# Window outputs of a hybrid encoder layer kept on chip, their norm and output projection begun in the last window units

## The chip, the core and the metric

The kernel runs on one core of one Trainium2 chip. TensorE (PE) does the matmuls, VectorE (DVE), ScalarE (ACT) and GpSimd (POOL) the elementwise work, SyncE (SP) issues most of the DMAs between HBM and the on-chip memories (SBUF, and PSUM where matmuls accumulate). The metric is device time in microseconds (us) of one execution, as a median of several runs.

## What is computed

One layer on 1024 tokens with 16 meta tokens ahead (L = 1040), width 1024, fp32. Two SwiGLU blocks stand around a mixer with two kinds of heads:

```
h += 0.5 * SwiGLU_1(RMSNorm(h))
z  = RMSNorm(h) @ W_in
     group A: 4 differential heads  a = softmax(q0 k0) - lam * softmax(q1 k1);  a @ v;  RMSNorm per head
     group B: sliding window (+-128 tokens, 16 meta keys), 8 query heads, 2 kv heads, a sink logit per head
h += concat(A, RMSNorm(B)) @ W_out
h += 0.5 * SwiGLU_2(RMSNorm(h));  out = RMSNorm(h)[16:]
```

The change lies in group B: its output (512 channels x 1024 tokens) has to be normed over its 512 channels, multiplied with the second half of W_out, and added to the residual h.

## The kernel before, in words

Each fp32 operand is cut into a rounded high part (a cast on ACT, L117) and a low part (a subtraction on DVE or POOL, L114), and a product is three matmuls, high by high, low by high and high by low (`mm3`, L163 to L169). Activations lie with channels on the 128 partitions and tokens along the free axis. A weight tile is loaded, cast and subtracted by `load_w` (L171). The order of instructions on each engine is not written out: when the program is built, a scheduler that plays a model timeline orders the engines' queues, within what pools and their buffers allow. So the text of the program and the order in a queue differ, and a pool with fewer buffers can hold work back.

The stages around the change, in time order:

- **Units** (L1019). 16 window units (2 kv heads x 8 token blocks of 128) are run with the projections that are still missing: `fillers` (L913) hands out projection matmuls (`pj`) between the unit's own. A unit is `win_scores` (L936: matmuls to `ws`, masked row maximum on DVE, exp on ACT to the tile `p4`, division on POOL) and, one unit later, `win_values` (L978: transposes to `wt`, cut into thi and tlo, matmuls with the values to `wo`, at L1007 and L1008 a copy and an addition to the output tile `ow`). L1009 writes `ow` to HBM, to the tensor `ow_d`. At i == 13 the projections are drained, the pools of differential heads opened, and `load_head(0)` (L728) loads head 0: keys and queries come from HBM (`kraw`, `qraw`), are cast on ACT and cut on POOL (`kl` L114, `qst` L743).
- **Head loop** (L1181). 4 differential heads x 8 query blocks are 32 steps, and 4 steps to drain. The first three score steps are drawn into units 14 and 15 (`EARLY`). A step is `scores` (L756: 12 matmuls `ds` for each of the two softmaxes, a row maximum on DVE L767, exp on ACT L769), `combine` one step later (POOL L776, DVE L777), `transposes` two steps later (`dt`, copied out on DVE and ACT), and on even steps from 4 on `values` (L1161). The odd steps from 9 on take one **tile** of `out_win` (L1128): 12 matmuls of 512 columns for one 128-row block m of the output and one half c of the tokens, of the window part of W_out, with the addition to h (`hrm`) and a write to `h2_d`. There are 16 such tiles, in the order m, then c; a weight block is loaded once for two tiles. 14 fit into the odd steps, two stand behind the loop.
- **Window norm** (`win_norm`, L1089), at step 4 for the first token half and at step 8 for the second: 1 MB is read back from `ow_d` into `own`, squared on ACT, summed over the four tiles by three additions on POOL (L1073), summed over partitions by one ones-matmul (L1075), then `rsqrt` (L1078; the activation function's table is exchanged for it and back), and four times a multiplication on POOL (L1095), a scaling on ACT (L1097) and a low part on DVE (L1098) give `ow_hi` and `ow_lo`.
- **Head norm** (`head_norm`, L1114) at steps 7, 11, 15, ... for half a head each.
- **Output projection** of the differential heads (`prepare2`, L1238): 16 tiles `po` of 12 matmuls, whose weight blocks 0 and 1 have buffers of the pool `owp`, open since before the loop; then the norm of the second FFN (`first_half`, `combine2`), beside which the first products of that FFN run (`lead`, L254, whose weights come by `rg<-wg`, L257).

Of the kernel before, what the change touches and what calls it, by code (L numbers as in the profile page):

```python
# [10 lines left out]
F32 = mybir.dt.float32  # L11
# [30 lines left out]
N_EARLY = sum(len(v) for v in EARLY.values())  # L42
DNG = 3
# [8 lines left out]
def layer(  # L52
# [10 lines left out]
    class Rings:  # L63
# [5 lines left out]
        def reserve(self, tag, bufs=1):  # L69
            pools = [self.stack.enter_context(mk_pool(f"{self.name}_{tag}{i}", side=self.side, space=self.space)) for i in range(bufs)]  # L70
            self.tags[tag] = [pools, 0]
            return self
# [650 lines left out]
    ow_d = dpool.tile([P, 4, SEQ], F32, name="ow_d")  # L723
# [4 lines left out]
    def load_head(hd):  # L728
        khs, kls, qs = [], [], []
        for c in range(2):  # L730
# [16 lines left out]
        v = kp.tile([P, NB + 1, P], F32, tag="v", name="v", bufs=2)  # L747
# [8 lines left out]
    def scores(head, qt, c, tiles, ds):  # L756
# [11 lines left out]
        p = dp.tile([P, L], F32, tag=f"dp{c}", name=f"dp{c}", bufs=3)  # L768
# [11 lines left out]
    pend, sc = {}, {}  # L780

    with ExitStack() as st:
# [63 lines left out]
        st_h.close()  # L846
        vpool2 = st.enter_context(mk_pool("vbp"))
# [130 lines left out]
        def win_values(kv, n, p4):  # L978
# [4 lines left out]
            for j in range(nk + 2):  # L983
# [22 lines left out]
            ow = wp.tile([P, 512], F32, tag="ow", name="ow")  # L1006
            nc.scalar.copy(tmp[mine, :], po[other, :])  # L1007
            nc.vector.tensor_tensor(ow[mine, :], po[mine, :], tmp[mine, :], op=ALU.add)  # L1008
            nc.sync.dma_start(  # L1009
                ow_d[mine, :, n * P : (n + 1) * P], ow[mine, :].rearrange("p (g q) -> p g q", g=4)  # L1010
# [8 lines left out]
        for i, (kv, n) in enumerate(units):  # L1019
# [5 lines left out]
            if i == 13:  # L1025
# [4 lines left out]
                for tag, bufs in (("v", 2), ("qst", 3), ("kh", 3), ("kl", 3), ("kraw", 1), ("qraw", 1)):  # L1030
                    kp.reserve(tag, bufs)
                dp = Rings(st_k, "dp", "right", bufs=2)
                for tag, bufs in (("dp0", 3), ("dp1", 3), ("at", 2), ("oh", 2)):
                    dp.reserve(tag, bufs)
# [15 lines left out]
    h2_d = [[dpool.tile([P, 512], F32, name=f"h2_{m}_{c}") for c in range(2)] for m in range(KT)]  # L1050
    st_o = ExitStack()
# [3 lines left out]
    owp = Rings(st_o, "ow").reserve("owraw").reserve("owhi", 2).reserve("owlo", 2)  # L1055
    with ExitStack() as st:
        op = Rings(st, "op").reserve("ow_hi").reserve("ow_lo")
        npool = Rings(st, "dn")
# [3 lines left out]
        ow_hi = op.tile([P, 4, SEQ], F32R, name="ow_hi")  # L1062
        ow_lo = op.tile([P, 4, SEQ], F32R, name="ow_lo")

        def sums(srcs, n):
            acc = npool.tile([P, 512], F32, tag="nacc", name="nacc")[:, :n]
            for i, s in enumerate(srcs):
                if i == 0:
                    nc.scalar.activation(acc, s, AF.Square)
                else:  # L1070
                    sq = npool.tile([P, 512], F32, tag="nsq", name="nsq")[:, :n]
                    nc.scalar.activation(sq, s, AF.Square)
                    nc.gpsimd.tensor_tensor(acc, acc, sq, op=ALU.add)  # L1073
            ps = psum.tile([P, 512], F32, tag="do", name="do")[:, :n]
            nc.tensor.matmul(ps, ones, acc, start=True, stop=True)  # L1075
            return ps

        def rsqrt(v, n, width):  # L1078
            r = npool.tile([P, SEQ], F32, tag="nr", name="nr")[:, :n]
# [318 lines left out]
```

## Time and profile before

| | us |
|---|---|
| median of 3 runs | 2109.07 |
| lowest, highest | 2106.53, 2112.87 |
| the profiled execution, its own time | 2112.15 |
| its span | 2110.4 |
| PE busy in the span | 1947.8 (92%) |
| DVE, POOL, ACT busy | 1304.6 (62%), 1042.0 (49%), 877.2 (42%) |
| mean granted TensorE clock | 0.974 of 2.4 GHz |

The page lists busy time for each engine over the whole span. It is an average over stages: the two FFNs take most of the span with PE near its limit, and PE's row of 40 slices shows its lowest full slices, 7 tenths, at slices 21 and 22 (1055 to 1161 us) and 27 and 28 (1372 to 1477 us), ahead of and behind the head loop. A stage is therefore read by itself: what each engine was busy in it, what the chain of waits names in it, and what single instructions wait for. The stages are the units (870 to 1043 us), a hand-over from the last units to step 9 of the head loop (1043 to 1151), the rest of that loop (to 1337), the output projection (to 1399) and the norm of the second FFN (to 1453). In a row of a timeline the first number is the start, the second the duration in us, and square brackets hold the idle time of the engine just before it and what ended it; 128x512 and the like are partitions x elements.

### The profile page before, as it was taken

The numbers are of one execution on the slowest core, as the hardware profiler recorded it, in microseconds if no ns is written. First come the engines' busy times: TensorE is split into PE (matmuls) and PEld (weight loads), VectorE is DVE, ScalarE is ACT, GpSimd is POOL, SyncE is SP. The second block draws the span as 40 slices with busy tenths as digits, with TensorE's granted clock in tenths as the row PEclk, the third lists the DMA queues.
The fourth block names the chain that finished last, engine by engine and source line by source line (L and its number), as shares of the span: only waits on it lengthen the run. The fifth ranks groups of instructions, "written<-read, shape, count | busy, mean of one in ns | idle before, by whom it ended". The sixth has DMA issues, their size and how long they took to land.

```text
span 2110.4 us, 30362 instructions
## 1 busy us (share of the span) xinstructions
PE 1947.8 (92%) x11484; PEld 1695.8 (80%) x11484; DVE 1304.6 (62%) x1804; ACT 877.2 (42%) x1609; POOL 1042.0 (49%) x856
## 2 busy tenths in 40 slices
PE   4799999998999999899977999877999999989998
PEld 4799999998999889777755777665788888867877
DVE  7865555547865572276667777478555555488745
ACT  5333333334532441266557666343333333344433
POOL 5655545444543651476457433036655545455453
PEclk9899999999999999999989999998999999999999
DMA  3232232327431452444442321522422332284222
GB/s 134 90 121 88 96 116 83 105 85 289 159 114 33 160 161 76 126 132 122 98 122 63 102 87 54 161 80 70 140 105 79 116 105 90 105 313 162 74 80 80
DMA packets 104563, 241.52 MB, mean 114 GB/s; under 512 B 14048, under 2 KB 28848, under 8 KB 104416
## 3 DMA queue, kind: packets, MB, share of 16 engines
q1 hardware_dynamic: 92896, 201.91, 30.3%
q0 software_dynamic: 11520, 37.67, 4.6%
q8 instruction: 90, 1.47, 0.3%
q14 instruction: 57, 0.47, 0.1%
HBM read 167.23 MB, written 65.44 MB: 110 GB/s over the span
## 4 chain that ended last, share of the span: by engine, by line
PE 70%; DVE 11%; DMA 6%; ACT 5%; POOL 3%; issue 3%; SPq 1%; DVEq 0%; POOLq 0%; ACTq 0%
PE p L226 37%; PE pA L557 8%; PE pC L557 4%; PE pj L167 4%; PE pv L867 3%; PE pd L167 2%; PE do L1166 2%; PE pB L557 2%; PE ds L763 2%; PE po L167 1%; DVE bl L114 1%; PE do L167 1%; PE wo L1000 1%; ACT dp L769 1%; PE wt L989 1%
## 5 line engine op out<-in xcount | busy, mean ns | idle before, releaser
L226 PE MATMUL p<-b_hi,wal 128*128 128x260 f32 (+1 forms) x528 | 146.5, 333 | 26.9 <-DVE wal L114 26.9
L226 PE MATMUL p<-b_hi,wah 128*128 128x260 f32 (+1 forms) x528 | 147.8, 334 | 13.2 <-ACT m L244 9.8
L226 PE MATMUL p<-b_lo,wah 128*128 128x260 f32 (+1 forms) x528 | 145.6, 331 | 7.7 <-DVE b_lo L114 7.7
L226 PE MATMUL p<-t_hi,wch 128*128 128x260 f32 (+1 forms) x528 | 140.5, 320 | 3.6 <-DVE u L114 3.6
L226 PE MATMUL p<-t_lo,wbh 128*128 128x260 f32 (+1 forms) x528 | 142.6, 320 | 0.0
L226 PE MATMUL p<-t_hi,wbh 128*128 128x260 f32 (+1 forms) x528 | 140.0, 321 | 1.5 <-ACT wbh L117 1.5
L226 PE MATMUL p<-t_lo,wch 128*128 128x260 f32 (+1 forms) x528 | 140.4, 320 | 0.0
L226 PE MATMUL p<-t_hi,wcl 128*128 128x260 f32 (+1 forms) x528 | 139.9, 319 | 0.0
L226 PE MATMUL p<-t_hi,wbl 128*128 128x260 f32 (+1 forms) x528 | 139.9, 320 | 0.0
L114 DVE TENSOR_TENSOR u<-p,m 128x520 f32<-128x520 f32 (+1 forms) x88 | 61.0, 693 | 111.2 <-PE p L226 107.4
L226 PEld LDWEIGHTS p<-b_hi,wal 128*128 128x128 f32 x528 | 92.2, 199 | 36.7 <-DVE wal L114 28.7
L117 ACT CAST wbh<-s 128x512 fp32r<-128x512 f32 x88 | 54.6, 621 | 156.2 <-PE p L226 149.4
L114 DVE TENSOR_TENSOR wal<-rg,wah 128x512 fp32r<-128x512 f32 x88 | 81.0, 922 | 61.9 <-ACT wah L117 61.8
L557 PE MATMUL pA<-bl,wh 128*128 128x260 f32 (+1 forms) x432 | 115.6, 322 | 1.6 <-DVE bl L114 1.6
L557 PE MATMUL pA<-bh,wh 128*128 128x260 f32 (+1 forms) x432 | 116.0, 323 | 1.0 <-DVE h L564 1.0
L114 DVE TENSOR_TENSOR bl<-r,bh 128x520 fp32r<-128x520 f32 (+1 forms) x126 | 111.3, 913 | 4.9 <-ACT bh L117 4.9
L117 ACT CAST wch<-ru 128x512 fp32r<-128x512 f32 x88 | 54.7, 622 | 143.4 <-PE p L226 72.9
L114 POOL TENSOR_TENSOR s<-ru 128x512 f32<-128x512 f32 x44 | 59.8, 1358 | 109.9 <-DVE wbl L114 90.7
L117 ACT CAST wah<-rg 128x512 fp32r<-128x512 f32 x88 | 54.1, 619 | 140.2 <-PE p L226 123.6
L557 PE MATMUL pA<-bh,wl 128*128 128x260 f32 (+1 forms) x432 | 112.2, 320 | 0.0
L226 PEld LDWEIGHTS p<-b_hi,wah 128*128 128x128 f32 x528 | 92.5, 199 | 24.1 <-ACT m L244 11.1
L564 DVE SCALAR_TENSOR_TENSOR h<-pA,h 128x520 f32<-128x520 f32 (+1 forms) x96 | 66.3, 692 | 68.1 <-PE pA L557 67.8
(288 smaller groups left out, 6099.1 us busy)
## 6 DMA issues: line engine op xcount, KB each, us to landing
rg<-wg SPq DMA_DIRECT2D x44, 512.0 KB, 3.6
ru<-wu SPq DMA_DIRECT2D x44, 512.0 KB, 5.3
wr<-wd SPq DMA_DIRECT2D x24, 768.0 KB, 4.4
r<-g_t SPq DMA_DIRECT2D x12, 780.0 KB, 6.0
r<-g_t SPq DMA_DIRECT2D x12, 768.0 KB, 5.8
g_b<-g POOLq DMA_DIRECT2D x27, 260.0 KB, 5.5
r<-g_b SPq DMA_DIRECT2D x9, 780.0 KB, 5.7
g_b<-g POOLq DMA_DIRECT2D x27, 256.0 KB, 5.3
```

Of the source, the lines that this page charges most:

```text
L114: eng.tensor_tensor(out, a, b, op=op)
L117: nc.scalar.copy(hi, src)
L167: nc.tensor.matmul(o, w, x[:, c0 : c0 + n], start=first and i == 0, stop=last and i == 2)
L226: nc.tensor.matmul(o, w_k(ww, k), x[:, k, c0 : c0 + cn], start=first and k == 0 and i == 0, stop=k == hk - 1 and i == 2, skip_group_check= ...
L557: nc.tensor.matmul(o, w_k(ww, k), xx[:, c0 : c0 + cn], start=new and k == 0 and q == 0, stop=k == DNG - 1 and q == 2, skip_group_check=not ...
L564: nc.vector.scalar_tensor_tensor(hs, full, 0.5, hs, op0=ALU.mult, op1=ALU.add)
L763: nc.tensor.matmul(o, qs[c][:, qt * P : (qt + 1) * P], kk[:, c0 : c0 + n], start=i == 0, stop=i == 1)
L769: nc.scalar.activation(p, full, AF.Exp, bias=mx, scale=-1.0, accum_out=z[:, c : c + 1])
L867: nc.tensor.matmul(ps[:m, 192 + c * 320 : 512 + c * 320], u[:, k, sl], w[:, k, c * 320 : (c + 1) * 320], start=k == 0 and i == 0, stop=k = ...
L989: nc.tensor.transpose(pt[:m, g * P : (g + 1) * P], p4[:, g, c0 : c0 + m], ident)
L1000: nc.tensor.matmul(po, vb[:m, vt, kv, :], t[:m, :], start=j == 1 and i == 0, stop=j == nk + 1 and i == 1)
L1166: nc.tensor.matmul(po[:, :256], v[:m, j, :], at[:m, j, :], start=j == 0, stop=j == NB)
```

## The change

- `ow_d` and its 16 writes and two reads are gone. Two tiles of the new pool `own` (one for each token half, 128 x 2048) are written by `win_values` directly. Later the same pool's buffers hold the differential heads' outputs `oh`.
- `win_norm(0)` stands behind `load_head(0)` at i == 13 of the units, when the first half of all window outputs is there (unit 11 was the last of it); `win_norm(1)` at step 1 of the head loop. The three POOL additions of each norm are gone; each of its four squares has a ones-matmul of its own that accumulates in PSUM. In the units its sums lie in the `ws` ring.
- `out_win` goes through c first, then m, so that the 8 tiles of the first token half come before those of the second. A weight block is then loaded and cut for each (m, c), 16 times instead of 8.
- `OUT_EARLY` draws one tile into unit 14 and two into unit 15; `OUT_STEPS` names the steps of the loop that take one: 2, 3, 5, 7, 9, 13, 17, 21, 25, 29, 33, 35, as far as an even step's place is not taken by `values`. Steps 11, 15, 19, 23, 27 and 31 have none. One tile stands behind the loop.
- `load_head(0)` cuts head 0's keys and queries on DVE; the other heads still on POOL. The head pools are opened smaller and extended behind the units. `p4` has 3 buffers instead of 4.
- In `prepare2` all 8 weight blocks have buffers of their own in `wp`, a pool opened there.

```diff
+OUT_EARLY = {14: 1, 15: 2}
+OUT_STEPS = (2, 3, 5, 7, 9, 13, 17, 21, 25, 29, 33, 35)
...
-    ow_d = dpool.tile([P, 4, SEQ], F32, name="ow_d")
...
-            split(kh, kl, kraw, nc.gpsimd)
+            split(kh, kl, kraw, eng)
             nc.scalar.copy(q, qraw)
-            nc.gpsimd.tensor_tensor(q[64:P, :], qraw[64:P, :], q[64:P, :].bitcast(F32), op=ALU.subtract)
+            eng.tensor_tensor(q[64:P, :], qraw[64:P, :], q[64:P, :].bitcast(F32), op=ALU.subtract)
...
+    def sums(srcs, n):
+        ps = out_ps()[:, :n]
+        for i, s in enumerate(srcs):
+            acc = npool.tile([P, 512], F32, tag="nacc", name="nacc")[:, :n]
+            nc.scalar.activation(acc, s, AF.Square)
+            nc.tensor.matmul(ps, ones, acc, start=i == 0, stop=i == len(srcs) - 1)
+        return ps
...
+    def out_win(m, c):
+        hi, lo = load_w(io["wout"][m][:, 4 * P :], owp, tag="ow", cols=4 * P, eng=nc.gpsimd)
...
+    def out_fill():
+        for c in range(2):
+            for m in range(KT):
+                yield from out_win(m, c)
...
-            p4 = wp.tile([P, 4, 400], F32, tag="p4", name="p4", bufs=4)
+            p4 = wp.tile([P, 4, 400], F32, tag="p4", name="p4", bufs=3)
...
-            ow = wp.tile([P, 512], F32, tag="ow", name="ow")
+            c0 = n % 4 * P
+            ow = owns[n // 4].rearrange("p (g q) -> p g q", g=4)[mine, :, c0 : c0 + P]
...
-            nc.sync.dma_start(
-                ow_d[mine, :, n * P : (n + 1) * P], ow[mine, :].rearrange("p (g q) -> p g q", g=4)
...
-                heads[0] = load_head(0)
+                out_ps = lambda: wps.tile([P, 512], F32, tag="ws", name="ws")
+                heads[0] = load_head(0, nc.vector)
+                win_norm(0, owp)
+                out = out_fill()
...
+            for _ in range(2 * OUT_EARLY.get(i, 0)):
+                next(out)
...
-            elif i >= 9:
-                work = fill
+            elif i in OUT_STEPS:
+                work = out
...
-            if i in (4, 8):
-                win_norm(i // 8)
+            if i == 1:
+                win_norm(1, op)
...
-                            io["wout"][m][:, : 4 * P], owp if m < 2 else wp, tag="ow", bufs=KT - 2, cols=4 * P
+                            io["wout"][m][:, : 4 * P], wp, tag="ow", bufs=KT, cols=4 * P
```

Where instructions stand in a queue before and after the change shows at three places. In these rows a line number is followed by the operation, what it writes and what it reads; line numbers of the changed program are higher by 10 to 20.

ACT, around the first score steps of head 0 (`dp_12579`, `dp_12596` are the exp of the first step's two softmaxes before, `dp_12613`, `dp_12630` after; `kh` and `qst` are casts of the head's keys and queries). Before:

```order
L117 CAST kh<-kraw 128x1040
L117 CAST thi<-wt 16x512
L1007 COPY otmp<-wo 64x512
L117 CAST thi<-wt 128x512
L742 CAST qst<-qraw 128x1024
L769 ACTIVATE dp_12596,dz<-ds,dmx_12594 128x1040
L117 CAST thi<-wt 128x512
L1007 COPY otmp<-wo 64x512
L769 ACTIVATE dp_12701,dz<-ds,dmx_12699 128x1040
L1069 ACTIVATE nacc<-own 128x512
L1072 ACTIVATE nsq<-own 128x512
L769 ACTIVATE dp_12712,dz<-ds,dmx_12710 128x1040
```

After:

```order
L801 ACTIVATE nacc<-own 128x512 x2
L129 CAST kh<-kraw 128x1040
L753 CAST qst<-qraw 128x1024
L780 ACTIVATE dp_12613,dz<-ds,dmx_12611 128x1040
L129 CAST owhi<-owraw 128x512
L129 CAST thi<-wt 128x512
L801 ACTIVATE nacc<-own 128x512 x2
L129 CAST thi<-wt 16x512
L1077 COPY otmp<-wo 64x512
L129 CAST thi<-wt 128x512
L780 ACTIVATE dp_12630,dz<-ds,dmx_12628 128x1040
L807 ACT_TABLE_LOAD
```

The squares of the first window norm (`nacc<-own`) and two casts of W_out blocks (`owhi`) stand ahead of and between the first exps now, and the table exchange of that norm right behind the first step's second exp; before, the first square stood behind the third exp.

PE, at the end of the head loop, from the last tiles of the window part (`do<-ow_hi, ow_lo`) to the first matmuls of the differential heads' projection (`po`). Before:

```order
L167 MATMUL do<-ow_hi,owhi 128x512
L167 MATMUL do<-ow_lo,owhi 128x512
L167 MATMUL do<-ow_hi,owlo 128x512
L167 MATMUL po<-o_hi,owhi 128x512
L167 MATMUL po<-o_lo,owhi 128x512
L1075 MATMUL do<-nacc,ones 128x512
L167 MATMUL po<-o_hi,owlo 128x512
L167 MATMUL po<-o_hi,owhi 128x512
```

After:

```order
L179 MATMUL do<-ow_hi,owhi 128x512
L179 MATMUL do<-ow_lo,owhi 128x512
L179 MATMUL do<-ow_hi,owlo 128x512
L179 MATMUL po<-o_hi,owhi 128x512
L179 MATMUL po<-o_lo,owhi 128x512
L179 MATMUL po<-o_hi,owhi 128x512
L179 MATMUL po<-o_lo,owhi 128x512
L179 MATMUL po<-o_hi,owlo 128x512
```

Before, the two first `po` matmuls stood ahead of the last ones-matmul, and 24 matmuls of window tiles followed ten more of them; now all `po` matmuls stand behind the last window tile.

SP, in the same stretch, where DMAs are issued (`h_7_1` is written by the last window tile, `h_0`, `h_1`, ... are the results of `po` tiles, `rg<-wg` the first weights of the second FFN). Before:

```order
L175 DMA owraw<-wout 128x512
L257 DMA rg_15701<-wg 128x512
L1134 DMA hrm<-h_d 128x512
L1251 DMA hd<-h_6_1_12853 128x512
L1263 DMA h_0_15001<-ha 128x512
L257 DMA rg_15729<-wg 128x512
L1141 DMA h_7_0_12854<-hrm 128x512
L257 DMA rg_15749<-wg 128x512
L1251 DMA hc<-h_7_0_12854 128x512
L257 DMA rg_15777<-wg 128x512
L175 DMA owraw<-wout 128x512 x2
L1141 DMA h_7_1_12855<-hrm 128x512
```

After:

```order
L1281 DMA h_2_15011<-hb 128x512
L1281 DMA h_3_15012<-hb 128x512
L269 DMA rg_15702<-wg 128x512
L1281 DMA h_4_15013<-hd 128x512
L269 DMA rg_15722<-wg 128x512
L1281 DMA h_5_15014<-hd 128x512
L1281 DMA h_6_15015<-hd 128x512
L269 DMA rg_15750<-wg 128x512
L1281 DMA h_7_15016<-hd 128x512
L269 DMA rg_15770<-wg 128x512
```

Before, four of the loads `rg<-wg` stood among the last window tiles, ahead of the writes of the first half's results but one; now the first stands among the writes of the second half's results, behind `h_3<-hb`.

## Rows read from the trace of the kernel before

**Rows 1.** Stages: length; busy PE, weight loads, DVE, ACT, POOL; clock, DMA share, GB/s.

```profile
870.00:1043.00 173.00, 165.36 (x890) 135.53 (x889) 110.52 (x228) 94.82 (x218) 111.89 (x93) 0.99 0.43 116
1043.00:1151.00 108.00, 77.22 (x382) 56.29 (x381) 77.67 (x100) 72.43 (x132) 63.07 (x41) 0.89 0.44 113
1151.00:1337.00 186.00, 170.67 (x870) 135.24 (x869) 126.82 (x152) 114.47 (x203) 67.41 (x45) 0.97 0.27 80
1337.00:1399.00 62.00, 57.44 (x234) 44.45 (x234) 35.41 (x50) 22.92 (x38) 6.88 (x5) 0.97 0.42 139
1399.00:1453.00 54.00, 31.40 (x98) 22.29 (x99) 49.50 (x49) 23.09 (x39) 31.93 (x20) 0.79 0.19 67
```

**Rows 2.** Pieces of the chain that ended last: start, us, what.

```profile
1081.70 7.99 DMA own<-ow_d
...
1171.06 0.87 PE do L1075 x2
...
1283.77 2.77 PE do L167 x12
```

**Rows 3.** DVE timeline, `combine` of steps 2, 8, 9, 31: start, duration, operation, idle before.

```profile
1103.57 1.30 DVE L777 SCALAR_TENSOR_TENSOR dp<-dp,drz,dp 128x1040 f32<-128x1040 f32 x1 [0.21 <-POOL dp L776]
...
1146.00 2.32 DVE L777 SCALAR_TENSOR_TENSOR dp<-dp,drz,dp 128x1040 f32<-128x1040 f32 x1 [1.43 <-POOL dp L776]
...
1151.19 1.29 DVE L777 SCALAR_TENSOR_TENSOR dp<-dp,drz,dp 128x1040 f32<-128x1040 f32 x1
...
1318.61 1.29 DVE L777 SCALAR_TENSOR_TENSOR dp<-dp,drz,dp 128x1040 f32<-128x1040 f32 x1
```

**Rows 4.** Timeline of DVE and POOL in the last units.

```profile
1051.44 2.34 POOL L816 TENSOR_TENSOR zs<-zs,sinT 128x1024 f32<-128x1024 f32 x1 [15.03 <-DMA zs<-z]
1051.50 3.36 DVE L817 TENSOR_TENSOR z<-z,cosT 128x1024 f32<-128x1024 f32 x1 [1.58 <-DMA zs<-z]
...
1056.61 1.35 DVE L818 TENSOR_TENSOR z<-z,zs 128x1024 f32<-128x1024 f32 x1
...
1058.40 2.44 POOL L114 TENSOR_TENSOR kl<-kraw,kh 128x1040 fp32r<-128x1040 f32 x1
```

**Rows 5.** Timeline of ACT, then DVE, behind the last unit.

```profile
1089.72 0.63 ACT L1069 ACTIVATE nacc<-own 128x512 f32<-128x512 f32 x1 [5.74 <-DMA own<-ow_d]
...
1092.01 0.17 DVE L774 RECIPROCAL drz<-dz 128x2 f32<-128x2 f32 x1 [4.88 <-ACT dp L769]
```

**Rows 6.** Groups by line, 1155 to 1345 us: count, busy us, mean ns, idle before.

```profile
L1097 ACT ACTIVATE ow_hi<-own,wgain 128x512 fp32r<-128x512 f32 x4 | 2.9, 720 | 1.8 <-POOL own L1095 1.8
...
L117 ACT CAST owhi<-owraw 128x512 fp32r<-128x512 f32 x7 | 4.3, 619 | 5.6 <-PE do L167 5.5
...
L1098 DVE SCALAR_TENSOR_TENSOR ow_lo<-own,wgain,ow_hi 128x512 fp32r<-128x512 f32 x4 | 3.7, 949 | 0.0
```

**Rows 7.** Timeline of ACT at a table exchange.

```profile
1150.77 1.28 ACT L769 ACT_TABLE_LOAD   x1
1152.07 1.13 ACT L769 ACTIVATE dp<-ds,dmx 128x1040 f32<-128x1040 f32 x1
```

**Rows 8.** Timeline at the output projection: SP, ACT, PE.

```profile
1352.01 0.86 SPq L175 DMA_DIRECT2D owraw<-wout  x2
...
1356.79 1.18 ACT L117 CAST owhi<-owraw 128x512 fp32r<-128x512 f32 x2 [4.93 <-DMA owraw<-wout]
...
1357.46 0.50 PE L167 MATMUL po<-o_hi,owhi 128*128 128x512 f32 x1 [2.08 <-ACT owhi L117]
```

**Rows 9.** Timeline of SP at the loads of `rg`, and of DVE at the FFN norm.

```profile
1342.44 0.33 SPq L257 DMA_DIRECT2D rg<-wg  x1
...
1405.30 2.27 DVE L114 TENSOR_TENSOR nacc<-nacc,nsq 128x512 f32<-128x512 f32 x3
1407.48 0.69 DVE L114 TENSOR_TENSOR wal<-rg,wah 128x512 fp32r<-128x512 f32 x1
...
1413.08 0.75 DVE L149 SCALAR_TENSOR_TENSOR hb<-hb,gains,nr 128x512 f32<-128x512 f32 x1
```

More of the change, by code (lines that the diff above doesn't have):

```diff
@@ L780, in layer @@
     pend, sc = {}, {}
+    h2_d = [[dpool.tile([P, 512], F32, name=f"h2_{m}_{c}") for c in range(2)] for m in range(KT)]
+    st_o = ExitStack()
+    owns, win_parts = [], {}
+    out_ps = None
+    def sums(srcs, n):
[5 more added lines that the diff above has]
+        return ps
@@ new lines, in rsqrt @@
+    def rsqrt(v, n, width):
+        r = npool.tile([P, SEQ], F32, tag="nr", name="nr")[:, :n]
+        nc.scalar.activation(r, v, AF.Abs_reciprocal_sqrt, bias=eps, scale=1.0 / width)
+        for c0 in range(0, n, 512):
+            vc, rc = v[:, c0 : c0 + 512], r[:, c0 : c0 + 512]
+            t = npool.tile([P, 512], F32, tag="nt", name="nt")
+            nc.scalar.activation(t, rc, AF.Square)
+            nc.vector.scalar_tensor_tensor(t, vc, EPS * width, t, op0=ALU.add, op1=ALU.mult)
+            nc.vector.scalar_tensor_tensor(rc, t, -3.0 * width, rc, op0=ALU.add, op1=ALU.mult)
+        return r
@@ new lines, in out_win @@
+    def out_win(m, c):
+        hi, lo = load_w(io["wout"][m][:, 4 * P :], owp, tag="ow", cols=4 * P, eng=nc.gpsimd)
+        o_hi, o_lo = win_parts[c]
+        c0, n = CH_REAL[c]
+        ht = owp.tile([P, 512], F32, tag="hrm", name="hrm")
+        nc.sync.dma_start(ht, h_d[m * P : (m + 1) * P, c0 : c0 + n])
+        ps = out_ps()
+        for k in range(4):
+            mm3([ps], w_k(hi, k), w_k(lo, k), o_hi[:, k, :], o_lo[:, k, :], ((0, n),), k == 0, k == 3)
+            if k == 1:
+                yield
+        tt(nc.vector, ht, ps, ht, ALU.add)
+        nc.sync.dma_start(h2_d[m][c], ht)
+        yield
@@ L846, in layer @@
         st_h.close()
+        own = Rings(st_o, "own").reserve("own", 2)
+        owns += [own.tile([P, 4 * 512], F32, tag="own", name="own") for _ in range(2)]
         vpool2 = st.enter_context(mk_pool("vbp"))
@@ L1054, in layer @@
     o_lo = opool.tile([P, 4, SEQ], F32R, name="o_lo")
-    owp = Rings(st_o, "ow").reserve("owraw").reserve("owhi", 2).reserve("owlo", 2)
     with ExitStack() as st:
-        op = Rings(st, "op").reserve("ow_hi").reserve("ow_lo")
-        npool = Rings(st, "dn")
+        op = Rings(st, "op").reserve("ow_hi1").reserve("ow_lo1").reserve("nv")
+        kp.extend(st, "left", v=1, qst=1, kh=1, kl=1)
+        at_pool = Rings(st, "at").reserve("at", 2)
         psum = Rings(st, "dps", space=PSUM).reserve("do").reserve("dt")
@@ L1060, in layer @@
         ds1 = Rings(st, "ds1", space=PSUM).reserve("ds")
[L1062 to L1076, printed above, removed]
@@ L1170, in values @@
             yield
-        def out_fill():
-            ws = {}
-            for m in range(KT):
-                for c in range(2):
-                    yield from out_win(m, c, ws)
-        fill = out_fill()
         ats, ohs = {}, {}
@@ L1203, in layer @@
                 if i % NB == 0:
[L1204 removed]
+                    if i // NB % 2 == 0:
+                        pair = own.tile([P, 4 * 512], F32, tag="own", name="oh")
+                    ohs[i // NB] = pair[:, i // NB % 2 * SEQ :][:, :SEQ]
             if i >= 4 and i % 2 == 0:
@@ L1230, in layer @@
                 head_norm(hd2, c, ohs[hd2])
-        for _ in fill:
+        for _ in out:
             pass
```

89 lines of the change are left out of this document (37 added, 52 removed).

## Prediction, made before the changed kernel was run

> **What bounds the kernel now.** I read the table of stages first [rows 1]. In the units PE is busy 165.4 of 173 us: work taken out of there is worth its full time, and work put in costs it. In the head loop from step 9 on PE is busy 170.7 of 186 us (92%), so PE bounds it too, though not by itself. Between them lies the hand-over, 108 us with PE busy 77.2 (71%), DVE 77.7 (72%), ACT 72.4 (67%) and the clock at 0.89: no engine is full, it is bound by chains. It leaves 30.8 us of PE idle. The chain of waits says which: the 1 MB read of the first window norm takes 7.99 us of it [rows 2], ACT sits 5.74 us in front of the first square, and the exp queued behind the square keeps DVE idle for 4.88 us [rows 5]. The output projection has 62 − 57.4 = 4.6 us without PE, the FFN norm 22.6 of 54 [rows 1]; there DVE is 92% busy and the bound.
>
> So the change takes window tiles from a stage where PE is nearly full and puts them where PE has 30.8 us free. Its worth is 'PE time saved in units, loop and tail' less 'what the hand-over and the FFN norm grow'.
>
> **The change part by part.** The profiled execution's own time is 2112.15 us, 3.08 above the median; the sum is made against it and then set on the median.
>
> *Units.* With `p4` in 3 buffers each unit's values come earlier against the next unit's scores, and six score matmuls, eight transposes and two value matmuls stand behind the last projection now. A tile of twelve 512-column matmuls takes 2.77 us [rows 2], 0.23 each; the sixteen are at most 3.7 us, and as most are narrower I take 2.6. They leave a stage at 96%: −2.6 (−1 to −3.7). The 16 writes of 128 KB leave SP's queue; nobody waited for them but the read named above.
>
> *Hand-over, to step 9.* Counted in the queues up to that step, this comes in. PE: 7 tiles (three in the units, four at steps 2, 3, 5, 7) x 2.77 = 19.4; six ones-matmuls more (four for each norm instead of one) x 0.87 [rows 2] = 5.2; the units' 2.6: together 27.2. DVE: head 0's four cuts, two inputs of 1024 to 1040 columns each, at 1.35 [rows 4] = 5.4; `ow_lo` of the second norm 4 x 0.95 [rows 6] = 3.8; seven additions at 0.69 (same shape, [rows 9]) = 4.8; that norm's two corrections 1.4; about eleven small operations of the late unit at 0.69 at most, 7.4: together 22.8. ACT: seven weight casts x 0.62 and four `ow_hi` x 0.72 [rows 6] = 7.2; two table exchanges x 1.28 [rows 7] = 2.6; two activations of 0.63 [rows 5] and about 4 of the unit: 15. POOL: eight cuts of weights in, six additions and four cuts of head 0 (2.44 each, [rows 4]) out, about level.
>
> Out go waits: the 5.74 and 4.88 us of [rows 5], parts of one stall, and head 0's cuts at 2.44 each, now 1.35. That stall hid nothing else of PE, so what comes next is whichever queue is longest. With the additions PE has 104.4 us, DVE 100.5 and ACT 87.4 to do. If PE reaches the loop's 92%, 108 us become 113.7 at the present clock; if the fuller queue lifts the granted clock from 0.89 to the loop's 0.97 [rows 1], its own 77.2 become 70.8, and the 98 us take 106.8. DVE at the FFN norm's 92% needs 109.6. The average of the three is 110; two full queues that feed each other do a little worse than one, so I take 111, +3. Lower end: 98 us at the units' 96%, 102.5 (−5.5). Upper end: 104.4 us at the 86% that PE has over the three stages from 1043 to 1399 (305.3 of 356), 121.7 (+14).
>
> *Head loop.* 14 tiles become 8: 6 x 2.77 = 16.6 us less of PE. One bound is that sum. The other comes from `combine`: steps 2 to 8, which hold no tile, take 42.4 / 6 = 7.07 us, steps 9 to 31, with one on every other step, 167.4 / 22 = 7.61 [rows 3]. Taking all eleven tiles out would by this give 22 x 0.54 = 11.9 us, and six of them 6.5. But the slow rate of steps 2 to 8 has two window norms, a head's load and the clock of the hand-over in it; the loop is then free of the second norm. I take −12 (−6.5 to −20, the last with some of that norm's tail behind step 9).
>
> *Tail and output projection.* One tile instead of two behind the loop: −2.8. The first weight block of the projection now lies where the last tile's operand lies, so its load waits for that tile's last matmul, and no tile is left to hide it. In the trace the same sequence runs from the issue of `owraw` at 1352.01 to the first matmul behind its cast at 1357.46 [rows 8]: 5.4 us, of which 2.08 were bare. It replaces the stage's 4.6 us of gaps, so +0.8: −2 together (−3 to +1).
>
> *FFN norm.* Before, the first weights `rg` were issued from 1342.44 on [rows 9], and cast and cut in the gaps of the tail. Now the loads stand on SP behind the writes of the second half's results, and five cuts of 0.69 [rows 9] fall on DVE ahead of or inside the second half's norm, 3.5 us. From the end of the last `nacc` to the first `hb` it took 1413.08 − 1407.57 = 5.5 us before [rows 9]; those cuts lie in that path, and PE has no other work there. I take +4 (+1, if the lead products fill the time as before, to +8, with a late load on top).
>
> Sum: −2.6 + 3 − 12 − 2 + 4 = −9.6. From 2112.15 that is 2102.5; on the median 2099.5.
>
> *Two rules weighed.* In the last units a DVE product of two SBUF inputs took 3.36 us beside a POOL product, and 1.35 by itself for the same shape [rows 4]. The Trainium skill ("SBUF — State Buffer", "Who interferes with whom") says that such a DVE instruction contends with a POOL instruction that reads SBUF, and that whoever came second blocks fully. That speaks against cutting head 0 on DVE beside POOL; the trace agrees, with those 2.0 us. Four cuts that all meet POOL would by it be 8 us more on DVE; at POOL's share here, 63 of 108 us [rows 1], 4.7, and the sum −5. A table exchange took 1.28 us, and the exp started within 0.02 us behind it [rows 7]. The Trainium skill ("ScalarE: Activation LUTs", "What ACT_TABLE_LOAD costs") puts a drain of 1.38 us beside the load, 2.66 in all; the row shows no such drain, and by the page ACT's 15 would be 18.
>
> **The rivals.**
> 1. *Slower: DVE becomes the bound of the hand-over.* It holds 100.5 us of work there. The other terms sum to −12.6, so the change is slower by 0.3% (6.3 us) once the hand-over grows by 19, to 127 us: when DVE gets no busier than 79%. For it: DVE is at 72% there and 64% in the units [rows 1], each row maximum stands on the chain of its step, and cuts of head 0, output additions and `ow_lo` now stand ahead of them in its queue. Against it: 92% in the FFN norm [rows 1], and most of what is added is not waited for at once. At 77% the stretch takes 130.5: +9.9, 2119.
> 2. *No change: the loop doesn't give PE's time back.* If steps without a tile fall to the 7.07 us of steps 2 to 8 and no lower, the loop gives 6.5; with the FFN norm at +6: −2.6 + 3 − 6.5 − 2 + 6 = −2.1, 2107. For it: steps 2 to 8 had no tile and were no faster. Against: the norms in them.
> 3. *The full gain.* The clock rises in the hand-over, which then gives 3 us, and the loop gives 16.6: −2.6 − 3 − 16.6 − 2 + 4 = −20, 2089.
> 4. *It doesn't do what it says.* If the tiles drawn early wait for the first norm until the units are over, they stand in the hand-over's second half and press on the steps there; that is rival 1 in another place and a part of its chance.
>
> **How the numbers follow.** A measurement of this kernel can tell about 0.3%, 6.3 us: faster is below 2102.7, slower above 2115.4. Forecast (2092 to 2102.7): 0.44. Full gain (below 2092): 0.14. No change (2102.7 to 2115.4): 0.28, half of it rival 2, the rest the forecast's own terms at their worse ends and DVE beside POOL. Slower: 0.14, mostly rival 1. So faster 0.58, same 0.28, slower 0.14. The hand-over's ends alone span −8.5 to +11 about its value, the loop's −8 to +5.5, the FFN norm's −3 to +4; as independent terms they give some −12 and +13, and with the rivals' tails 2083 to 2116 leaves out 0.06 below and 0.13 above.
>
> **What would show it.** In the changed kernel's stages: units about 2 to 3 us shorter; hand-over to step 9's `combine` between 103 and 122 us with PE above 85% and the clock above 0.89; no wait for `own` by DMA; steps 9 to 31 at about 7.1 us; one gap of about 5 us on PE ahead of the first `po`, ended by the cast of `owhi`; the second half's norm 3 to 5 us later behind the last `po` than before. The prediction is wrong if the row maxima of steps 0 to 8 sit behind cuts or low parts on DVE (rival 1), if the loop's steps stay at 7.5 (rival 2), or if the FFN norm starts over 8 us later.

## The result, and the profile after

The changed kernel takes 2140.06 us (median of 4 runs, 2137.61 to 2144.57), the kernel before 2110.97 in the same comparison: a ratio of 1.014, interval 1.011 to 1.017. I had forecast 2099.5 with a range from 2083 to 2116. It is slower by about 30 us where a gain of 10 was expected. One execution each of e9 and e11 below had a mean granted clock of 0.84 and 0.65, and the times given leave it out.

The two profiled executions are 2112.15 and 2144.57 us, 32.4 apart. Three marks cut the stretch that changed: the end of the last projection matmul `pj`, the `combine` of step 9, and the `combine` of step 31; the last `po` matmul ends it. The table of busy time between the marks, before:

```profile
1042.80:1151.20 108.40, 77.62 (x385) 56.69 (x383) 78.06 (x101) 72.83 (x132) 63.07 (x41) 0.89 0.44 113
1151.20:1318.60 167.40, 154.48 (x802) 123.35 (x800) 121.20 (x145) 109.94 (x194) 66.15 (x44) 0.98 0.26 77
1318.60:1398.50 79.90, 72.96 (x300) 56.11 (x301) 40.33 (x58) 27.25 (x47) 7.64 (x5) 0.96 0.41 134
```

and after (columns as in [rows 1]: length, busy PE, weight loads, DVE, ACT, POOL, granted clock, DMA share, GB/s):

```profile
1038.90:1179.30 140.40, 116.01 (x513) 85.16 (x511) 92.25 (x130) 85.57 (x156) 65.11 (x47) 0.87 0.42 113
1179.30:1351.70 172.40, 141.46 (x715) 111.78 (x714) 114.82 (x134) 106.87 (x188) 55.04 (x39) 0.93 0.15 44
1351.70:1432.60 80.90, 71.09 (x288) 54.98 (x286) 38.65 (x57) 26.85 (x45) 10.88 (x6) 0.91 0.40 133
```

The projections end 3.9 us earlier. The hand-over grows by 32.0 us, from 108.4 to 140.4. The head loop, which by its matmuls holds 5 window tiles between its marks instead of 12 (step 9's now stands ahead of the first mark), gets 5.0 us longer, and PE's clock in it falls from 0.98 to 0.93. Tail and projection take 1.0 us more, and what is behind them 1.7 less (710.2 of span instead of 711.9). Together 32.4.

In the hand-over DVE went from 72% to 66% and ACT from 67% to 61%; PE went from 72% to 83%, at a lower clock, and stays well below the 92% of the loop before. So no engine's queue ran out of time. PE's busy time grew by 38.4 us and its idle time fell by 6.4 only, from 30.8 to 24.4: what was added did not, taken together, go into the gaps. The PE timeline shows a wait at unit 14 (`ws<-kxh`: the unit's score matmuls):

```profile
1044.81 0.34 PE L1014 MATMUL ws<-kxh,wqs 128*128 128x400 f32 x1
...
1060.10 1.91 PE L802 MATMUL ws<-nacc,ones 128*128 128x512 f32 x2
...
1073.39 0.45 PE L1014 MATMUL ws<-kxh,wqs 128*128 128x400 f32 x1 [1.03 <-DVE nt L812]
```

Unit 14's first score starts at 1044.81 and its second at 1073.39, released by DVE's `nt`, the operation that reads the window norm's sums. Before, the last of unit 15's scores started at 1049.03. The window's scores, the norm's sums and the early tiles take the same PSUM tag, `ws`, with two buffers, in the order of the program: sums, unit 14's four scores, a tile, unit 15's four scores, two tiles. The sums hold a buffer until the squares, the ones-matmuls, the reciprocal root and `nt` are done; three of unit 14's scores and all of unit 15's stand behind that. The last unit's output, on DVE, before and after:

```profile
1082.76 0.69 DVE L1008 TENSOR_TENSOR ow<-wo,otmp 64x512 f32<-64x512 f32 x1
```

```profile
1112.14 0.69 DVE L1078 TENSOR_TENSOR own<-wo,otmp 64x512 f32<-64x512 f32 x1 [0.29 <-ACT otmp L1077]
```

In the program the head loop's PSUM pools take the place of the units', and its first transposes begin beside the last unit's output, at 1109.59 instead of 1085.09. That this space is what they wait for is read from the program; no row names it. The chain of waits of the kernel after has window tiles on it in full (start, us, what); the granted clock was 0.81 in the first of them and 0.66 in the second, which makes them longer than the 2.77 us of [rows 2]:

```profile
1088.30 3.42 PE ws L179 x12
...
1124.12 4.41 PE do L179 x12
...
1140.01 2.69 PE do L179 x11
```

Behind the second of these tiles stands a score, and its row maximum (`dmx`) stands on DVE behind the tile's addition, for which DVE waits, and a low part:

```profile
1128.55 0.69 DVE L126 TENSOR_TENSOR hrm<-do,hrm 128x512 f32<-128x512 f32 x1 [3.29 <-PE do L179]
1129.16 1.77 DVE L824 SCALAR_TENSOR_TENSOR ow_lo<-own,wgain,ow_hi 128x512 fp32r<-128x512 f32 x1
1130.85 1.23 DVE L778 TENSOR_REDUCE dmx<-ds 128x1 f32<-128x1040 f32 x1
```

Before, the waits of scores for an exp were the largest part of PE's idle time in the hand-over, 11.7 us. The longest is the one behind the first norm's square:

```profile
1092.03 1.23 PE L763 MATMUL ds<-kh,qst 128*128 128x264 f32 x3 [4.19 <-ACT dp L769]
```

### The profile page after: what moved, and what is told of

It is laid out like the page before. It is cut to its first block, busy times and chain, and to the rows that moved or that the text cites. A ratio compares the mean times of both kernels' runs of the same rounds, so it can differ in the third digit from the quotient of the medians.

```text
span 2142.8 us, 30369 instructions
## 1 busy us (share of the span) xinstructions
PE 1967.7 (92%) x11496; PEld 1707.8 (80%) x11496; DVE 1315.5 (61%) x1808; ACT 886.0 (41%) x1619; POOL 1038.3 (48%) x854
## 4 chain that ended last, share of the span: by engine, by line
PE 74%; DVE 11%; ACT 5%; DMA 4%; issue 3%; POOL 1%; SPq 1%; DVEq 0%; ACTq 0%; POOLq 0%
PE p L238 38%; PE pA L569 7%; PE pj L179 5%; PE pC L569 4%; PE do L1189 3%; PE pv L936 3%; PE ds L774 3%; PE pd L179 2%; PE po L179 2%; DVE bl L126 2%; PE pB L569 2%; PE do L179 1%; PE wo L1069 1%; ACT dp L780 1%; PE wt L1058 1%
## 5 line engine op out<-in xcount | busy, mean ns | idle before, releaser
L126 POOL TENSOR_TENSOR s<-ru 128x512 f32<-128x512 f32 x44 | 58.3, 1325 | 116.8 <-DVE wbl L126 89.0
```

Of the source, the lines that this page charges most:

```text
L126: eng.tensor_tensor(out, a, b, op=op)
```

## Experiments

Two questions were open: what holds the hand-over, and why a loop with six tiles less is not shorter. The marks for all kernels, in us. 'Unit' is the last unit's output and 'step 9' the `combine` of step 9, both counted from the end of the last `pj` (1042.8 us in the kernel before, 1038.9 after); 'loop' is `combine` 9 to 31; 'tail' from there to the last `po`; 'ratio' is against the kernel before on the same chip, with its interval. 'Tiles' counts the window tiles, by their matmuls, ahead of step 9's `combine`, in the loop and in the tail. The marks are read from the timelines of DVE and PE, from one execution of each kernel. Where two kernels have the same queues up to a mark, they show the scatter: at step 9, 0.2 us between the kernel before and e4, 0.9 between e8 and e9, but 2.9 at step 8 between the kernel after and e5. A difference below 3 us ahead of step 9 is therefore not read from one pair. Times on different chips are compared by their ratios: the median of the kernel before lay between 2107.5 and 2111.0 us.

| kernel | time | unit | step 9 | loop | tail | tiles | ratio |
|---|---|---|---|---|---|---|---|
| before | 2111.0 | 39.9 | 108.4 | 167.4 | 79.9 | 0, 12, 4 | |
| after | 2140.1 | 73.2 | 140.4 | 172.4 | 80.9 | 8, 5, 3 | 1.014 (1.011 to 1.017) |
| e1 | 2140.7 | 62.2 | 136.1 | 170.2 | 81.2 | 8, 5, 3 | 1.013 (1.010 to 1.017) |
| e2 | 2154.8 (1 run) | 63.5 | 129.4 | 175.2 | 94.0 | 5, 5, 6 | |
| e3 | 2119.9 (1 run) | 64.6 | 120.1 | 162.0 | 87.5 | 1, 11, 4 | |
| e4 | 2143.1 (1 run) | 40.0 | 108.1 | 178.5 | 107.3 | 0, 6, 10 | |
| e5 | 2128.7 | 71.2 | 135.4 | 159.2 | 80.5 | 7, 6, 3 | 1.010 (1.008 to 1.012) |
| e6 | 2119.2 | 63.7 | 116.8 | 161.9 | 87.5 | 1, 11, 4 | 1.006 (1.004 to 1.008) |
| e7 | 2110.6 | 51.2 | 105.8 | 171.6 | 84.6 | 0, 12, 4 | 1.002 (1.001 to 1.003) |
| e8 | 2114.0 | 51.8 | 114.4 | 162.1 | 85.8 | 1, 11, 4 | 1.002 (1.001 to 1.004) |
| e9 | 2109.8 | 51.9 | 115.3 | 161.5 | 82.8 | 1, 11, 4 | 1.001 (0.999 to 1.002) |
| e10 | 2109.4 | 50.1 | 114.5 | 162.3 | 78.2 | 2, 11, 3 | 1.000 (0.999 to 1.002) |
| e11 | 2107.6 | 50.4 | 106.5 | 169.0 | 77.0 | 1, 12, 3 | 0.9995 (0.998 to 1.001) |
| e12 | 2114.5 | 51.2 | 130.5 | 162.8 | 63.7 | 4, 11, 1 | 1.002 (1.001 to 1.003) |

**e1: the first norm behind unit 15's scores.**

```diff
-                win_norm(0, owp)
-                out = out_fill()
...
+            if i == 15:
+                win_norm(0, owp)
+                out = out_fill()
-OUT_EARLY = {14: 1, 15: 2}
+OUT_EARLY = {15: 3}
```

> The changed kernel with the first window norm written behind unit 15's scores instead of behind unit 13, and its three early tiles behind it; all work stays in the hand-over. Theory R (ring): the norm's sums hold one of the two ws buffers in PSUM, so three of unit 14's four scores and all of unit 15's wait for the norm's chain; the units end late, and the loop's PSUM opens only behind them. Then the last unit's output moves from 1112 us to about 1085 to 1090, step 9's combine from 1179 to about 1155, and the time falls by 18 to 26 us, to about 2116. Rival W (work): the queues of DVE, ACT and PE hold too much in that stretch. The same work is still there, so step 9 stays at 1172 or later and the time within 7 us of the changed kernel's 2140.

The last score of unit 15 went from 1093.5 to 1063.5 us and the last unit's output from 73.2 to 62.2, so the ring did hold them. But step 9 came only 4.3 us earlier and the time not at all: a miss for the price that I had put on it. The norm and three tiles still stood ahead of the steps, and step 9 and the time lie where rival W had put them.

**e2: no early tiles; e3: the old fill.** Both without tiles in the units; e2 has the first of these edits only and keeps the four tiles on steps 2, 3, 5 and 7, e3 has both and tiles on all odd steps from 9 on.

```diff
-OUT_EARLY = {14: 1, 15: 2}
+OUT_EARLY = {}
-OUT_STEPS = (2, 3, 5, 7, 9, 13, 17, 21, 25, 29, 33, 35)
+OUT_STEPS = tuple(range(9, 36, 2))
```

> The changed kernel without the three tiles drawn into units 14 and 15; they go behind the loop (four tiles there, +8.3 us of PE at the end). Theory R: the units wait for the norm's sums and only a little for tiles: the last unit's output comes 3 to 6 us earlier than 1112, since one tile stood in the ring between the units' scores; the time is 2138 to 2146. Rival W: 8.3 us of PE, 1.9 of ACT and 2.1 of DVE less in the hand-over; step 9 comes 8 us or more earlier without the last unit's output being much earlier, the time is about 2138.

> The changed kernel with no early tile and with tiles on all odd steps from 9 on, as before the change: 14 tiles in the loop, two behind it. Theory C (chain): a loop step lasts as long as its score, maximum and exp chain lets it, tiles fill PE's waits; steps 9 to 31 take 165 to 173 us although six tiles more stand in them, and the time falls below the changed kernel's by the tiles that left the hand-over, to 2120 to 2132. Rival P (PE-bound loop, the prediction's): six tiles more cost the loop 12 to 16 us, steps 9 to 31 take 184 or more, the time is 2140 to 2150.

From after to e2 step 9 comes 10.9 us earlier, from e2 to e3 another 9.3. So the seven tiles cost the hand-over 20.3 us, 2.9 each: their whole PE time, though PE had been idle for 31 us there. e2's own time is worse than expected: the three more tiles behind its loop cost 13.1 us there instead of 8.3, and in this one run all that is behind the last `po` took 5.4 us more than in the kernel after. e3's loop has six tiles more than after's, and is 10.4 us shorter, 3 us below what theory C allowed. Rival P, the PE-bound loop of the prediction, is out; why more tiles make the loop shorter, C doesn't say.

**e4: the kernel before, with its loop thinned.**

```diff
-            elif i >= 9:
+            elif i >= 9 and i % 4 == 1 or i == 35:
                 work = fill
```

> The kernel before the change, with tiles only on steps 9, 13, 17, 21, 25, 29, 33 and 35: 8 in the loop, 8 behind it instead of 2. Theory C: steps 9 to 31 still take 164 us or more (167.4 before), and the six tiles behind the loop add 16.6 us and their weight loads' gaps: 2125 to 2135. Rival P: the loop gets 12 to 16 us shorter (152 to 156), the time is 2109 to 2117.

The loop without six tiles takes 178.5 us, 11.1 more than with them. That is against P, and within C's '164 or more', but a step that gets longer is not what C's reason gives. The tail grows by 27.4 us, 4.6 for each tile there, and the time, 2143.1 us, lies above both ranges.

**e5: as many tiles in the loop, on other steps.** Before, each odd step had a tile; the change left them on steps 9, 13, 17, ... and took them from 11, 15, 19, ..., which are the steps with a head norm.

```diff
-OUT_STEPS = (2, 3, 5, 7, 9, 13, 17, 21, 25, 29, 33, 35)
+OUT_STEPS = (2, 3, 5, 7, 11, 15, 19, 23, 27, 31, 33, 35)
```

> The changed kernel, but its six loop tiles of steps 9 to 29 stand on the other odd steps, 11, 15, 19, 23, 27 and 31, where a head norm exchanges ACT's table; the number of tiles in the loop and all else stay. Theory H (cover): the loop got no shorter because the head norms' steps lost the tile that PE worked on while ACT exchanges its table and PE waits for an exp. Then steps 9 to 31 fall from 172 to 158 to 163 us and the time by 8 to 14, to about 2129. Rival K (clock and chain): with fewer tiles anywhere PE has more gaps, the granted clock is lower, and the steps' chain is the bound wherever the tiles stand: 169 us or more, time within 4 us of 2140.

The loop falls from 172.4 to 159.2 us, as theory H said, and the ratio from 1.014 to 1.010, which is 8 us, with intervals that just overlap. Between the marks e5 has one tile more than the kernel after, because step 9's tile stands ahead of the mark there; it also puts e5's step 9 5.0 us earlier, with 2.9 us of scatter in that. The loops' rows in the table of windows, e4, e5, e3:

```profile
1146.80:1325.30 178.50, 145.84 (x731) 114.61 (x729) 119.55 (x141) 110.27 (x193) 57.86 (x41) 0.94 0.16 48
```

```profile
1176.50:1335.70 159.20, 139.49 (x729) 109.61 (x727) 113.60 (x135) 105.68 (x189) 59.51 (x40) 0.98 0.17 50
```

```profile
1157.50:1319.50 162.00, 148.84 (x786) 119.19 (x784) 119.79 (x138) 107.15 (x192) 66.92 (x45) 0.99 0.25 75
```

PE is idle for 19.7 us in e5's loop and 32.7 in e4's, and the clock is 0.98 against 0.94. What happens on such a step stands in the timeline. A head norm exchanges ACT's table only where a reciprocal root is taken: between the marks at steps 11, 19 and 27, with the second halves of heads 0 to 2, and in the kernel after, e1, e2 and e4 at step 31 too. At steps 15 and 23 there is none, so H had two of its six places wrong. In the kernel after, step 19, no tile:

```profile
1253.16 1.28 ACT L780 ACT_TABLE_LOAD   x1
...
1255.72 1.24 PE L774 MATMUL ds<-kh,qst 128*128 128x264 f32 x3 [3.78 <-ACT dp L780]
...
1258.47 2.77 PE L1189 MATMUL do<-at,v 128*128 128x256 f32 x8
```

In e3, the same head norm, with a tile on its step:

```profile
1230.18 1.89 PE L1189 MATMUL do<-at,v 128*128 128x256 f32 x8
...
1230.76 1.28 ACT L807 ACT_TABLE_LOAD   x1
...
1232.95 1.89 PE L1189 MATMUL do<-at,v 128*128 128x256 f32 x8
...
1236.60 0.74 PE L774 MATMUL ds<-kh,qst 128*128 128x264 f32 x3 [0.69 <-ACT dp L780]
```

The head norm exchanges ACT's table, and the next exp starts behind the second exchange. In the kernel after, PE's next matmul in order is a score that waits for that exp: 3.78 us of idle time, and behind it the eight value matmuls take 2.77 us at a clock of 0.68 instead of 1.89 at 1.00. In e3 the scheduler has put the value matmuls of the step into that time. The tile's own matmuls do not fill the gap: step 19's ran ahead of it there, until 1226.6. Nor does the tile fix the order. e5's step 27 has one, puts only eight value matmuls into the gap and waits; e4's step 11 has none, and the values stand in the gap:

```profile
1308.22 0.74 PE L774 MATMUL ds<-kh,qst 128*128 128x264 f32 x3 [2.54 <-ACT dp L780]
```

```profile
1166.08 1.99 PE L1166 MATMUL do<-at,v 128*128 128x256 f32 x8 [0.99 <-ACT nv L1122]
...
1171.87 0.75 PE L763 MATMUL ds<-kh,qst 128*128 128x264 f32 x3 [0.90 <-ACT dp L769]
```

But order and tile mostly go together. The two steps around such an exchange (`combine` 10 to 12, 18 to 20, 26 to 28) take 21.6 to 22.9 us in ten of the twelve cases without a tile on the step (after, e1, e2, e4), and 16.5 to 20.9 in all but one of the 30 with one (the other ten kernels; the one is e5's step 27, 22.5). Together the three take 66.2 us in the kernel after and 55.7 in e3, which is the whole difference of their loops. So the loop was lengthened by the order at three exchanges. Why the scheduler chooses it when the step has no tile stays open.

**e6: head 0's cuts on POOL again**, on top of e3.

```diff
-                heads[0] = load_head(0, nc.vector)
+                heads[0] = load_head(0, nc.gpsimd)
```

> The changed kernel with the old fill (as e3_old_fill) and head 0's four cuts back on POOL. If cutting on DVE beside POOL costs the hand-over (the contention weighed in the prediction), step 9 comes 2 to 5 us earlier than e3's 1157.5 and the time is 2115 to 2118; if it shortens the way to the first scores, as its first combine at 1071 instead of 1083 suggests, step 9 comes 2 us later or more and the time is 2121 to 2126.

Step 0's `combine` is 9.3 us later after the last `pj`, step 9 3.3 us earlier as the first case had it, and the time the same (2119.2 and 2119.9), which was in neither. So no effect of the engine that cuts head 0 shows in the time.

**e7 and e8: the norms in the loop.** e3's fill with the norms at steps 3 and 8 (e7, the diff) or in the same way at 0 and 2 (e8); their sums then have the loop's `do` tile.

```diff
-                win_norm(0, owp)
...
-            if i == 1:
-                win_norm(1, op)
+            if i in (3, 8):
+                win_norm(i // 8, (owp, op)[i // 8])
```

> The old fill, and both window norms in the head loop again, at steps 3 and 8 (before the change 4 and 8), with the window outputs still kept on chip. Theory R: the norm's sums in the units' ring are what holds the last units; the last unit's output comes back from 1102 to 1080 to 1086, step 9 from 1157.5 to 1146 to 1152 (before 1151, with the read from HBM), and the time is 2107 to 2114, the tail's 7 us left over. Rival: the units are late because p4 has three buffers or for head 0's cuts; the last unit's output stays at 1095 or later.

> As e7, with the norms at steps 0 and 2 of the loop's text, so earlier in the queues but with their sums in the loop's own PSUM tile. Theory R: the last unit's output at 1080 to 1090 as in e7. If the norms' ACT and DVE work ahead of the first steps costs them, step 9 is 3 to 8 us later than in e7 and the time that much higher; if only the ring did harm, the two are within 3 us.

Theory R holds. In e7 the last unit's output comes at 51.2 us instead of 64.6 and step 9 at 105.8, which is 2.6 us earlier than before the change, within the scatter: the read of [rows 2, 5] is gone, the units are still 11 us later, and the two about cancel.

```profile
1140.26 1.29 DVE L788 SCALAR_TENSOR_TENSOR dp<-dp,drz,dp 128x1040 f32<-128x1040 f32 x1
```

e8 has step 9 8.6 us later and its loop 9.5 us shorter: the second norm and step 9's tile are only moved from one side of the mark to the other. Against e3, whose norms stand at unit 13 and step 1, e8's step 9 comes 5.7 us earlier; that is the price of the norm in the units' ring. Unit 15's last score still is late: it starts 25.3 us behind the last `pj` in e7, 6.2 in the kernel before. In e7's PE queue two of its four scores stand behind the first scores of head 0, which wait 3.67 and 1.12 us for DVE's cuts of the queries; before, all four stood ahead of them. Whether `p4` with three buffers brings that order about is not shown; no two kernels here differ in that alone.

**e9 to e12: the tail, and tiles ahead of step 9.** e9 is e8 with the first two weight blocks of the projection loaded and cut ahead of the last window tiles. e10 adds a tile on step 7; e11 does both on e7; e12 is e10 with tiles on steps 3 and 5 too (the diff's last line; in e10 and e11 the range alone).

```diff
+        wpre = own.tile([P, 4 * 512], F32R, tag="own", name="wpre")
+        for m in range(2):
+            raw = owp.tile([P, 4 * P], F32, tag="owraw", name="owraw")
+            nc.sync.dma_start(raw, io["wout"][m][:, : 4 * P])
+            hi, lo = (wpre[:, (2 * m + x) * 512 : (2 * m + x + 1) * 512] for x in range(2))
+            split(hi, lo, raw)
+            ws_pre[m] = hi, lo
         for _ in out:
             pass
...
+OUT_STEPS = (3, 5, *range(7, 36, 2))
```

> e8 with the first two weight blocks of the output projection loaded and cut ahead of the last window tiles, into a buffer of the pool own that is free by then (the head outputs of heads 0 and 1 are normed). Tests the tail: in e8 PE waits 4.69 us for the cast of the first of these blocks and 2.16 us for the norm's correction. If that wait is on the path, the stretch from step 31's combine to the last po matmul falls from 85.8 to 80 to 82 us and the time by 3 to 6 us, to about 2109; if the blocks behind it are late anyway, by less than 2.

> e9 with one tile more in the loop, on step 7, where the first head norm stands, and one less behind it. Theory H (a tile on a head norm's step fills PE's wait at the table exchange): step 9 comes at most 1 us later and the tail is 3 to 4.5 us shorter, the time 2 to 4 us below e9. Rival: a tile in the hand-over costs its 2.7 us or more there as the seven of the change did (22 us in all); the time is within 2 us of e9 or above.

> e7 (norms at steps 3 and 8) with the early weight blocks and the tile on step 7. e7 and e8 came out 2110.6 and 2114.0; with both repairs the tail is 6 to 9 us shorter than e7's 84.6 and the time 2103 to 2107, below the kernel before the change by 0.1 to 0.3%. If the second norm at step 8 and the tile on step 7 stand in each other's way, step 9 or 10 is 3 us or more later and the time 2108 or more.

> e10 (norms at steps 0 and 2, early weight blocks, tile on step 7) with tiles on steps 3 and 5 too; all 16 tiles stand in the loop's text then and none behind it. In the changed kernel the seven tiles ahead of step 9 cost 20 us there, 2.9 each. If that was the tiles' own price in the hand-over, step 9 comes 5 to 6 us later after the last projection matmul than in e10 (114.5 us) and the tail gives back at most that: time 2108 to 2112. If they were dear only because the norm's sums and the tiles shared the units' ring, step 9 comes less than 2.5 us later and the time is 2103 to 2107.

e9's tail is 3.1 us shorter than e8's, less than the 4 to 6 expected: the wait of 4.69 us was on the path, but waits of 1.53 and 2.25 us for other casts of these weights come in its place. The ratio falls from 1.002 to 1.001, 3 us, with intervals that overlap. In the kernel after this wait is the largest gap of the tail (PE timeline):

```profile
1385.95 0.80 PE L179 MATMUL po<-o_hi,owhi 128*128 128x512 f32 x1 [4.91 <-ACT owhi L129]
```

In e10 the tile on step 7 costs the hand-over nothing (115.3 and 114.5) and the tail is 4.6 us shorter; but the time differs by only 0.4. It says nothing for theory H, for the norm on step 7 exchanges no table. e11 comes to 0.9995 of the kernel before, interval 0.998 to 1.001: equal, not better. In e12 the two tiles on steps 3 and 5 cost 16.0 us ahead of step 9, 8 each, more than either theory said; the tail, with two tiles less, gives 14.5 of it back, and the time is 2114.5, above both ranges. Its chain shows how a tile costs more than its matmuls:

```profile
1130.03 2.80 PE do L179 x12
...
1135.79 3.62 DMA h<-hrm
...
1139.43 0.33 SPq L834
...
1141.93 5.57 DMA qraw<-qa_d
...
1148.78 1.12 PE dt L1172 x4
```

L834 is the load of h for a later tile. It needs one of two buffers, which is free only when an earlier tile has been written (`h<-hrm`), so it waits on SP, and head 1's loads of keys and queries stand behind it on the same queue. The casts that wait for these loads stand in ACT's queue ahead of the next exp: none starts between 1130.03 and 1148.63 us. e10's chain has the same loads on it, but two exps run while they are under way, at 1136.41 and 1143.04. So the 2.9 us of a tile in the changed kernel is no constant.

## Why the prediction was wrong

The step that failed is the hand-over's: that 27 us of added work on PE would go into its 31 us of idle time there, and that only a full engine could stop it. The runs showed the seven tiles lengthening the stretch by their whole length, 20.3 us, and PE's idle time falling by 6.4.

- **Units, −2.6:** 3.9 us earlier in these two executions, which shows nothing: e4, with the queues of the kernel before, ends its projections at 1038.6 us instead of 1042.8, and the changed kernels end them between 1034.5 and 1043.8. But the step behind it failed. I saw sixteen matmuls of a unit slide behind the last projection and put them down to `p4` and to 2.6 us of work. Later scores of the same units stood behind the norm's sums in a ring of two PSUM buffers, and what slid was not work but the end of a chain of score, maximum, exp, division, transposes and values. The program has the sums ahead of unit 14's scores; I read the count of what moved and not what it waited for.
- **Hand-over, +3 (−5.5 to +14):** +32.0, and this is the main miss. I asked which engine gets full. None did. In steps, by the runs, each to some 3 us: output kept on chip and the late unit, −2.6 (e7); the second norm and step 9's tile ahead of the mark, +8.6 (e8, and given back in the loop); the norms at unit 13 and step 1, +5.7 (e3); four tiles on steps 2 to 7, +9.3 (e2); three tiles in the units, +10.9. PE's idle time there was spent inside chains: 11.7 of 30.8 us were scores waiting for the exp that frees their PSUM, 9.7 matmuls and transposes of the window outputs waiting for casts and cuts. In the kernel after the first kind is down to 1.4 us, so work did stand there. But a score behind a tile starts later, its row maximum too, and other waits came in: 3.4 us for the cuts of the queries, 3.3 for low parts, 2.4 for the norm's `nt`. The chain of waits lists tiles with their full length. It need not be so for every tile: e10's on step 7 cost nothing.
- **Head loop, −12 (−6.5 to −20):** +5.0. I took 0.39 to 1 us of loop for each us of tile taken out, without asking which steps lose theirs. On plain steps a tile costs the loop something: e5 has five fewer than e3 there and is 2.8 us shorter, 6.8 without what it lost at step 27's exchange, so 0.6 to 1.4 each. At the three exchanges the order that came without a tile cost 10.6 us against e3. Against the kernel before, the steps around them are 8.2 us longer and all others together 3.2 shorter, where I had put −12. The comparison that I used, steps 2 to 8 against 9 to 31, could not show it.
- **Tail, −2 (−3 to +1):** +1.0, at the range's end; the gap in front of `po` was 4.91 us, where I had taken 5.4 for the whole sequence from load to matmul in place of 4.6 us of gaps. What I missed is that a tile behind the loop costs 4.4 to 4.6 us and not 2.77 (e2, e4, e10).
- **FFN norm, +4 (+1 to +8):** −1.7 for all that is behind the last `po`, which lies between 708.8 and 717.1 us in the fourteen kernels. The cuts of the late `rg` did fall into the norm, as I had said, but the first `hb` came 14.2 us behind the last `po` instead of 14.6. They ran while DVE waited for others, and I had added them up as if it never did.
- **The two rules weighed.** The four DVE cuts beside POOL were to cost up to 8 us, an estimate from the 2.0 us of [rows 4]. The 1.35 us there were not 'by itself', for POOL's divisions ran beside it from 1055.15 to 1058.43. In the kernel after, the two cuts for head 0's first half took 1.55 and 1.51 us, and the other two, with POOL idle, 1.24 and 1.22; the four divisions on POOL beside the first two took 5.33 us, 3.28 before. The Trainium skill ("SBUF — State Buffer", "Who interferes with whom") says that a DVE instruction with two SBUF inputs contends with a POOL instruction that reads SBUF. The trace agrees, with some 0.3 us a cut on DVE and 2 us on POOL, and e6 shows no time moved by it. The Trainium skill ("ScalarE: Activation LUTs", "What ACT_TABLE_LOAD costs") puts a drain of 1.38 us beside a table's load. It is not seen after the change either: the exchange at 1253.16 takes 1.28 us and the exp starts at 1254.45.
- **The rivals.** Rival 1 had the side and the place right, and two thirds of the size (130.5 us for the hand-over, 140.4 measured), but not the mechanism: DVE's share fell. Its sign, row maxima behind low parts, shows on the chain at 1130.85, on a DVE that was not full. Rival 2's sign showed too, with steps of 7.8 us in the loop, but by the exchanges and not by a rate of steps without tiles. Rival 4 was nearest, that early tiles wait and press on the steps; I counted it as a part of rival 1 instead of asking what the tiles and the norm hold while they wait. A chance of 0.14 for slower was too low for a change that puts seven tiles and a norm on a stretch bound by chains.

## What to carry to other kernels

Idle time on an engine is only room for more work if the idle time isn't a link of the chain that sets the end: find what the engine waits for there, and what a new instruction, queued in order, will make wait. Work taken out of a stage also changes the order of what is left, here which matmuls stand behind a table exchange; after it is taken out, look at what each long wait is covered by. When a new user takes a buffer from a ring, count the buffers and follow how long it holds one: a ring of two with one long holder serves everyone else one at a time.

## What the runs showed of the hardware

Gaps on PE came with a lower granted clock, which makes them dearer. In the loop the clock was 0.98 to 0.99 where PE was idle for 8 to 12% of the time (before, e3, e5) and 0.93 to 0.94 where it was idle for 18% (after, e4). Right behind a wait of 3.78 us it was 0.50, the lower of its two levels, and 0.68 in the eight value matmuls that followed; they took 2.77 us, and 1.89 in e3 at a clock of 1.00. A window tile took 4.41 us at a clock of 0.66 where it takes 2.77 at 1.00. Such a wait is paid twice, once as idle time and once in the matmuls behind it.
